# Two-layer hybrid decoder on one core: up projection of the feed-forward part by four feature tiles at a time instead of two

## The chip, the cores and the metric

One core of a Trainium2 chip runs the whole kernel. The metric is the device time of one execution in microseconds (us), the median of the timed runs. Engines: PE is TensorE's matmul, PEld its weight load, DVE VectorE, ACT ScalarE, POOL GpSimd, SP SyncE, which issues the DMAs.

## The reference

Two layers act on a residual stream x of 256 tokens by 2048 features, all in float32. In each layer x gets the output of a mixer (three kinds of attention), then that of a cross attention, then that of the feed-forward part, in which the change lies:

```python
h = rms_norm(x, ffn_norm[l])
u = h @ ffn_w_up[l]                       # 2048 x 11008
up = jnp.pad(u, ((0, 0), (CONV_WIDTH - 1, 0), (0, 0)))
cw = ffn_conv_w[l]
uc = (cw[0] * up[:, :-2] + cw[1] * up[:, 1:-1] + cw[2] * up[:, 2:] + ffn_conv_b[l])
g, val = jnp.split(uc, 2, axis=-1)
x = x + (jax.nn.silu(g) * val) @ ffn_w_down[l]   # 5504 x 2048
```

## The kernel before

Products are made in a rounded float32 format in three parts. A weight piece is loaded by SP into a buffer of tag `raw`; ACT rounds it to `hi` (L98) and DVE subtracts to get `lo` (L100), both in `halves`, called from `load_split`. There are four `raw`, four `hi` and three `lo` buffers of 1 MB each, so a piece's `lo` can be written once PE has left the piece three before it. The activations lie split in the same way: a tile `h3[k]` holds, for one of 16 k-tiles (KT) of 128 features, 256 columns of rounded tokens and 256 of the rest. A matmul of `hi` with all 512 columns (L283) and one of `lo` with the first 256 (L285) make the three parts.

Up projection has 86 feature tiles of 128 in each layer (NF = 43 gates and 43 values). `up_acc` makes the sums of two tiles at a time in two banks of the pool tag `mm` (`pmm`, four banks; the other four have the tag `at`, `pat`). A piece holds 8 k-tiles by 256 columns (`EIGHTS`); for each k-tile come two hi matmuls, then two lo. One k-tile of two feature tiles is called a step below, and 8 steps use up a piece. After every four k-tiles `tick` lets waiting generators run (small sums of the norm factor, parking, weight sums), in an order that counts ticks.

`up_tiles` reads the sums: ACT copies one half of the bank (L1189), DVE adds the other (L1192) and multiplies by the norm factor R (L1193), ACT applies the last convolution tap and the bias (L1194), DVE the two other taps (L1195, L1197). `gate` applies silu on ACT (L1205) and multiplies gate and value on DVE (L1206) into a tile of two neighbouring feature tiles, a pair. For 13 of the pairs (`SEVEN`) down projection uses a seven-product scheme. Such a pair is parked: DVE makes differences (L316 to L318), ACT and DVE round and split (L305, L306, two of each for a pair) and SP writes four tiles to DRAM (L324). For the same pairs `add_up` loads weights of the down projection (L334), DVE adds them (L338) and SP writes the sums to DRAM (L342), paced over the up stage by `todo`. `fetch` later loads a parked pair and one sum again (L355, L359), and is called twice near the end of the up stage, then once for each such pair in `down` (products at L375 to L377, weights at L384 to L386 and L405).

Each engine's instructions are ordered by a scheduler when the program is built; that order is fixed on the chip. Tiles of the tag `k` (`slot`, 38 buffers) hold activations and loads, those of the tag `t` (`tmp`, 7) short-lived values.

## Time and profile before

| What | us |
|---|---|
| median of 3 timed runs | 2463.83 (2463.75 to 2463.97) |
| the profiled execution, its own time | 2463.87 |
| its span, first to last instruction | 2462.1 |
| PE busy in the span | 2454.1 |
| DVE busy | 2009.5 |
| ACT busy | 1414.0 |
| up projection, first layer, about | 537 to 1016 |

The up stage of the second layer lies at about 1760 to 2238 us, and down projection follows each. A busy time is the union of an engine's instructions; matmuls overlap in the record, so the distance from one start to the next, and not the length of one, tells their pace. The same holds for DVE and ACT, whose instructions overlap by some 0.08 us. Idle time of an engine counts only where the chain that ended last goes through it.

### The profile page before, as it was taken

The numbers are of one execution on the slowest core, as the hardware profiler recorded it, in microseconds if no ns is written. First come the engines' busy times: TensorE is split into PE (matmuls) and PEld (weight loads), VectorE is DVE, ScalarE is ACT, GpSimd is POOL, SyncE is SP. The second block draws the span as 40 slices with busy tenths as digits, with TensorE's granted clock in tenths as the row PEclk, the third lists the DMA queues.
The fourth block names the chain that finished last, engine by engine and source line by source line (L and its number), as shares of the span: only waits on it lengthen the run. The fifth ranks groups of instructions, "written<-read, shape, count | busy, mean of one in ns | idle before, by whom it ended". The sixth has DMA issues, their size and how long they took to land.

```text
span 2462.1 us, 35930 instructions
## 1 busy us (share of the span) xinstructions
PE 2454.1 (100%) x13288; PEld 2110.8 (86%) x13288; DVE 2009.5 (82%) x3190; ACT 1414.0 (57%) x1860; POOL 156.2 (6%) x170
## 2 busy tenths in 40 slices
PE   9999999999999999999999999999999999999999
PEld 8788888898888888888887888888988888888887
DVE  7886767778888887899968877776888888878898
ACT  6555566465555555566655555655555555556664
POOL 2301101010000000000031011010100000000000
PEclk9999999999999999999999999999999999999999
DMA  8555556469999898898964555564799999988996
GB/s 281 169 179 162 167 168 221 167 195 319 298 298 315 292 301 263 298 377 293 352 208 154 172 171 159 170 219 141 233 309 301 302 300 304 300 259 314 349 344 240
DMA packets 465444, 619.39 MB, mean 252 GB/s; under 512 B 21182, under 2 KB 334068, under 8 KB 465268
## 3 DMA queue, kind: packets, MB, share of 16 engines
q1 hardware_dynamic: 465268, 617.10, 75.4%
q8 instruction: 104, 1.70, 0.3%
q14 instruction: 72, 0.59, 0.1%
HBM read 558.30 MB, written 58.72 MB: 251 GB/s over the span
## 4 chain that ended last, share of the span: by engine, by line
PE 98%; DVE 1%; issue 0%; DMA 0%; ACT 0%; SPq 0%; POOL 0%; POOLq 0%
PE mm L283 31%; PE mm L285 16%; PE mm L247 10%; PE mm L252 10%; PE mm L248 10%; PE mm L375 4%; PE mm L376 4%; PE mm L377 4%; PE at L376 2%; PE at L377 2%; PE at L375 2%; PE at L690 1%; PE mm L281 1%; PE mm L280 1%; PE at L789 0%
## 5 line engine op out<-in xcount | busy, mean ns | idle before, releaser
L100 DVE TENSOR_TENSOR lo<-raw,hi 128x2048 fp32r<-128x2048 f32 (+4 forms) x466 | 994.5, 2136 | 268.1 <-PE mm L252 109.1
L98 ACT ACTIVATE hi<-raw 128x2048 fp32r<-128x2048 f32 (+4 forms) x466 | 825.5, 1774 | 521.4 <-PE mm L248 198.7
L283 PE MATMUL mm<-k,hi 128*128 128x512 f32 x3008 | 946.1, 396 | 0.0
L285 PEld LDWEIGHTS mm<-k,lo 128*128 128x128 f32 x3136 | 584.9, 188 | 133.5
L285 PE MATMUL mm<-k,lo 128*128 128x256 f32 x3136 | 616.5, 278 | 0.0
L283 PEld LDWEIGHTS mm<-k,hi 128*128 128x128 f32 x3008 | 458.4, 189 | 0.4 <-DVE k L208 0.2
L247 PE MATMUL mm<-hi,k 128*128 128x512 f32 (+2 forms) x1152 | 431.2, 374 | 1.2 <-ACT hi L98 0.8
L248 PE MATMUL mm<-hi,k 128*128 128x512 f32 (+2 forms) x1152 | 423.5, 368 | 0.0
L252 PE MATMUL mm<-lo,k 128*128 128x512 f32 (+2 forms) x1148 | 422.0, 368 | 0.3 <-DVE lo L100 0.3
L247 PEld LDWEIGHTS mm<-hi,k 128*128 128x128 f32 x1152 | 216.8, 188 | 38.5 <-issue 4.8
L252 PEld LDWEIGHTS mm<-lo,k 128*128 128x128 f32 x1148 | 216.0, 188 | 36.9 <-DVE lo L100 0.7
L248 PEld LDWEIGHTS mm<-hi,k 128*128 128x128 f32 x1152 | 217.2, 189 | 32.0
L1194 ACT ACTIVATE t<-t,cw 128x256 f32<-128x256 f32 x172 | 94.3, 595 | 134.1 <-DVE t L1193 134.1
L1195 DVE SCALAR_TENSOR_TENSOR t<-t,cw 128x255 f32<-128x255 f32 x172 | 81.8, 480 | 30.9 <-ACT t L1194 30.9
L375 PE MATMUL mm<-hi,a 128*128 128x512 f32 x272 | 106.2, 390 | 0.4 <-DVE k L419 0.4
L376 PE MATMUL mm<-hi,a 128*128 128x512 f32 x272 | 105.8, 389 | 0.0
L377 PE MATMUL mm<-lo,a 128*128 128x512 f32 x272 | 100.2, 389 | 0.0
L338 DVE TENSOR_TENSOR k<-k 128x512 f32<-128x512 f32 x104 | 69.3, 687 | 24.7 <-DMA k<-in_ffn_w_down_dram 24.0
L1197 DVE SCALAR_TENSOR_TENSOR t<-t,cw 128x254 f32<-128x254 f32 x172 | 81.8, 480 | 3.0
L375 PE MATMUL at<-hi,k 128*128 128x512 f32 x208 | 80.9, 389 | 0.0
L376 PE MATMUL at<-hi,k 128*128 128x512 f32 x208 | 80.9, 389 | 0.0
L283 PE MATMUL mm<-a,hi 128*128 128x512 f32 x256 | 80.8, 396 | 0.0
(247 smaller groups left out, 2854.0 us busy)
## 6 DMA issues: line engine op xcount, KB each, us to landing
raw<-in_ffn_w_up_dram SPq DMA_DIRECT2D x168, 1024.0 KB, 6.1
raw<-in_w_in_dram SPq DMA_DIRECT2D x152, 512.0 KB, 4.7
k<-parked SPq DMA_DIRECT2D x184, 256.0 KB, 6.1
k<-in_ffn_w_down_dram SPq DMA_DIRECT2D x156, 256.0 KB, 6.5
raw<-in_ffn_w_down_dram SPq DMA_DIRECT2D x32, 1024.0 KB, 7.4
raw<-in_ffn_w_down_dram SPq DMA_DIRECT2D x56, 512.0 KB, 6.3
summed<-k SPq DMA_DIRECT2D x104, 256.0 KB, 3.9
parked<-a SPq DMA_DIRECT2D x104, 256.0 KB, 5.0
```

The costliest lines, as they stand in the source:

```text
L98: rounded[0] = nc.scalar.activation(hi[:, v, :], src[:, v, :], AF.Copy)
L100: nc.vector.tensor_tensor(lo[:, v, :], src[:, v, :], hi[:, v, :].bitcast(F32), OP.subtract)
L247: nc.tensor.matmul(o, lhsT=xh, rhs=hi[:, j, :], start=first, stop=False)
L248: nc.tensor.matmul(o, lhsT=xl, rhs=hi[:, j, :], start=False, stop=False)
L252: ins = nc.tensor.matmul(o, lhsT=xh, rhs=lo[:, j, :], start=False, stop=last)
L283: nc.tensor.matmul(outs[i], lhsT=w[0][i], rhs=acts[k], start=first, stop=False)
L285: ins = nc.tensor.matmul(own[i], lhsT=w[1][i], rhs=acts[k][:, :S], start=False, stop=last and (i == 1 or not whole))
L375: nc.tensor.matmul(bank[q], lhsT=x[0], rhs=w[0], start=first, stop=False)
L376: nc.tensor.matmul(bank[q], lhsT=x[1], rhs=w[0], start=False, stop=False)
L377: return nc.tensor.matmul(bank[q], lhsT=x[0], rhs=w[1], start=False, stop=left[q] == 0)
L1194: nc.scalar.activation(v, u, AF.Identity, scale=cw[:, 2, f:f + 1], bias=cw[:, 3, f:f + 1])
L1195: nc.vector.scalar_tensor_tensor(v[:, 1:], u[:, :S - 1], cw[:, 1, f:f + 1], v[:, 1:], op0=OP.mult, op1=OP.add)
```

## The change

Up projection goes by four feature tiles. A weight piece has four k-tiles by 512 columns, 1 MB as before. For each k-tile there are four hi matmuls, then four lo. The gate tiles of a group of four use the four `mm` banks, its value tiles the four `at` banks, in turn. Evacuated gates wait for their values in `k` tiles instead of `t` tiles. Groups start at tiles 0, 4, ..., 36; the pair 40 and 41 and the last tile 42 keep pieces of 8 k-tiles by 256 columns. Pacing of `add_up` is called before the gates and before the values of a group. `fetch` is called after tile 41 rather than 39.

```diff
-        def up_sums(fs):
-            return fs, up_acc(up, [(fs[0] * P, 2 * P)] if fs[1] == fs[0] + 1 else [(f * P, P) for f in fs], h3)
-
-        def up_tiles(fs, outs):
+        def up_sums(fs, new):
+
+            n = len(fs)
+            runs = [(fs[0] * P, n * P)] if fs[-1] == fs[0] + n - 1 else [(f * P, P) for f in fs]
+            outs = [new() for _ in fs]
+            for k0 in range(0, KT, 16 // n):
+                m = 16 // n
+                hi, lo = load_split([up[:, k0:k0 + m, c:c + w] for c, w in runs], m, n * P)
+                for j in range(m):
+                    k = k0 + j
+                    for i in range(n):
+                        nc.tensor.matmul(outs[i], lhsT=hi[:, j, i * P:(i + 1) * P], rhs=h3[k], start=k == 0, stop=False)
+                    for i in range(n):
+                        ins = nc.tensor.matmul(outs[i][:, :S], lhsT=lo[:, j, i * P:(i + 1) * P], rhs=h3[k][:, :S],
+                                               start=False, stop=k == KT - 1)
+                    if (j + 1) * n % 8 == 0:
+                        tick(ins)
+            return fs, outs
+
+        def up_tiles(fs, outs, new=tmp):
 
             res = []
-            uvs = [tmp() for _ in fs]
+            uvs = [new() for _ in fs]
...
-        for f in range(0, NF - 1, 2):
-            while todo and (total - len(todo)) * (NF - 5) < total * (f + 2):
+        def pace(f):
+            while todo and (total - len(todo)) * (NF - 5) < total * f:
                 step(add_up(dn, *todo.pop(0)))
-            us = [up_sums([f, f + 1])]
+
+        for f in [*range(0, NF - 4, 4), NF - 3, NF - 1]:
+            fs = list(range(f, min(f + 4 if f < NF - 3 else f + 2, NF)))
+            pace(f + 2)
+            if len(fs) == 1:
+                gs = up_tiles(*up_sums([f, NF + f], pmm))
+                gate(f, *gs)
+                break
+            us = up_sums(fs, pmm)
             if f:
-                gs = up_tiles(*us.pop())
-            us.append(up_sums([NF + f, NF + f + 1]))
+                gs = up_tiles(*us, new=slot)
+            pace(f + 4)
+            vs = up_sums([NF + v for v in fs], pat)
             if not f:
-                gs = up_tiles(*us.pop(0))
-            vs = up_tiles(*us.pop())
-            gate(f, gs[0], vs[0])
-            gate(f + 1, gs[1], vs[1])
-            if f == NF - 5:
+                gs = up_tiles(*us, new=slot)
+            vs = up_tiles(*vs)
+            for v, a, b in zip(fs, gs, vs):
+                gate(v, a, b)
+            if f == NF - 7:
                 wanted.extend((i, g) for g in range(D // GW) for i in pairs_of(g) if i in SEVEN)
+            if f == NF - 3:
                 for _ in range(2):
                     fetch()
-        gs = up_tiles(*up_sums([NF - 1, 2 * NF - 1]))
-        gate(NF - 1, gs[0], gs[1])
```

Before and after, each engine has the same number of instructions. Three places in the built order show what moves. In the changed program the up matmuls are L1192 (hi) and L1194 (lo), the evacuation L1205 and L1208 to L1213, and the gate's product L1222. Numbers in names tell buffers' uses apart.

PE, in the middle of the up stage of the first layer, one k-tile and the start of the next, before:

```order
L283 MATMUL mm_6729<-k_5261,hi_6783 128x512
L283 MATMUL mm_6730<-k_5261,hi_6783 128x512
L285 MATMUL mm_6729<-k_5261,lo_6784 128x256
L285 MATMUL mm_6730<-k_5261,lo_6784 128x256
L283 MATMUL mm_6729<-k_5262,hi_6783 128x512
L283 MATMUL mm_6730<-k_5262,hi_6783 128x512
```

and in the changed program:

```order
L1192 MATMUL mm_6709<-k_5179,hi_6777 128x512
L1192 MATMUL mm_6710<-k_5179,hi_6777 128x512
L1192 MATMUL mm_6711<-k_5179,hi_6777 128x512
L1192 MATMUL mm_6712<-k_5179,hi_6777 128x512
L1194 MATMUL mm_6709<-k_5179,lo_6778 128x256
L1194 MATMUL mm_6710<-k_5179,lo_6778 128x256
L1194 MATMUL mm_6711<-k_5179,lo_6778 128x256
L1194 MATMUL mm_6712<-k_5179,lo_6778 128x256
```

The matmul's width changes after every four instead of every two, and four banks take turns instead of two.

DVE, where pair 5 (tiles 10 and 11) is gated and parked, before:

```order
L1206 TENSOR_TENSOR k_6718<-t_6704,t_6612 128x256
L1197 SCALAR_TENSOR_TENSOR t_6705<-t_6705,cw_132 128x254
L100 TENSOR_TENSOR lo_6890<-raw_6887,hi_6889 128x2048
L1206 TENSOR_TENSOR k_6718<-t_6705,t_6613 128x256
L316 TENSOR_TENSOR t_6753<-k_6718 128x256
L317 TENSOR_TENSOR t_6753<-t_6753,k_6718 128x128
L306 TENSOR_TENSOR a_6774<-k_6718,a_6773 128x512
L318 TENSOR_TENSOR t_6753<-k_6718,t_6753 128x128
L338 TENSOR_TENSOR k_6723<-k_6723,k_6724 128x512
L306 TENSOR_TENSOR a_6806<-t_6753,a_6805 128x512
L338 TENSOR_TENSOR k_6725<-k_6725,k_6724 128x512
L100 TENSOR_TENSOR lo_6955<-raw_6952,hi_6954 128x2048
```

and in the changed program, where pairs 4 and 5 (`k_6693` and `k_6698`) are gated together, from the last gate on:

```order
L1222 TENSOR_TENSOR k_6698<-t_6668,k_6460 128x256
L306 TENSOR_TENSOR a_6760<-k_6693,a_6759 128x512
L316 TENSOR_TENSOR t_6739<-k_6698 128x256
L306 TENSOR_TENSOR a_6768<-k_6698,a_6767 128x512
L317 TENSOR_TENSOR t_6739<-t_6739,k_6698 128x128
L338 TENSOR_TENSOR k_6703<-k_6703,k_6704 128x512
L318 TENSOR_TENSOR t_6739<-k_6698,t_6739 128x128
L338 TENSOR_TENSOR k_6705<-k_6705,k_6704 128x512
L306 TENSOR_TENSOR a_6800<-t_6735,a_6799 128x512
L100 TENSOR_TENSOR lo_6876<-raw_6873,hi_6875 128x2048
L306 TENSOR_TENSOR a_6808<-t_6739,a_6807 128x512
L100 TENSOR_TENSOR lo_6952<-raw_6949,hi_6951 128x2048
```

Before, a weight piece's L100 stands between the evacuation of two tiles and their park; in the change the evacuation of four tiles, four gates, both parks but one instruction and a weight sum stand between one L100 and the next. The L100 ahead of these rows is that of the third piece after the group whose sums are read.

SP, at the end of the up stage of the first layer, from the last weight pieces on, before:

```order
L222 DMA raw_10023<-in_ffn_w_up_dram 128x8x128 x2
L405 DMA raw_10080<-in_ffn_w_down_dram 128x2x1024
L355 DMA k_9753<-parked_5895 128x512
L355 DMA k_9754<-parked_5897 128x512
L355 DMA k_9755<-parked_5929 128x512
L355 DMA k_9756<-parked_5931 128x512
L359 DMA k_9761<-summed_5507 128x512
```

and in the changed program, some rows further on:

```order
L386 DMA raw_10207<-summed_5515 128x512
L384 DMA raw_10258<-in_ffn_w_down_dram 128x1024
L385 DMA raw_10258<-in_ffn_w_down_dram 128x512
L386 DMA raw_10258<-summed_5691 128x512
L355 DMA k_9962<-parked_5897 128x512
L355 DMA k_9963<-parked_5899 128x512
L355 DMA k_9964<-parked_5931 128x512
L355 DMA k_9965<-parked_5933 128x512
L359 DMA k_9970<-summed_5509 128x512
```

The loads of the first parked pair move from behind down's first weight piece to behind its fifth, `raw_10258`, which takes the buffer of the first, `raw_10080`, once that one is split.

## Rows read from the trace of the kernel before

**Rows 1.** The head of the page: the span, and busy time, share of the span and instructions of each engine.

```profile
span 2462.1 us, 35930 instructions
...
PE 2454.1 (100%) x13288; PEld 2110.8 (86%) x13288; DVE 2009.5 (82%) x3190; ACT 1414.0 (57%) x1860; POOL 156.2 (6%) x170
```

**Rows 2.** Windows inside the up stage of the first and of the second layer: start and end, length, then busy time and instructions of PE, PEld, DVE, ACT and POOL, the granted clock, the DMA engines' share and GB/s.

```profile
541.00:1014.00 473.00, 473.00 (x2721) 412.79 (x2720) 403.30 (x605) 264.02 (x329) 1.74 (x1) 1.00 0.91 298
...
1764.00:2130.00 366.00, 366.00 (x2106) 319.47 (x2105) 313.17 (x470) 203.32 (x251) 1.75 (x1) 1.00 0.92 302
```

**Rows 3.** The chain of work that ended last, shares of the span by engine and by line.

```profile
PE 98%; DVE 1%; issue 0%; DMA 0%; ACT 0%; SPq 0%; POOL 0%; POOLq 0%
PE mm L283 31%; PE mm L285 16%; PE mm L247 10%; PE mm L252 10%; PE mm L248 10%; PE mm L375 4%; PE mm L376 4%; PE mm L377 4%; PE at L376 2%; PE at L377 2%; PE at L375 2%; PE at L690 1%; PE mm L281 1%; PE mm L280 1%; PE at L789 0%
```

**Rows 4.** Groups by line and shape, 545 to 1010 us, the two up matmuls: count, busy us, mean ns of one, idle us of the engine before them.

```profile
L283 PE MATMUL mm<-k,hi 128*128 128x512 f32 x1333 | 418.9, 395 | 0.0
L285 PE MATMUL mm<-k,lo 128*128 128x256 f32 x1334 | 262.1, 278 | 0.0
```

**Rows 5.** Timeline of PE in the up stage: start us, length of the merged row, instruction, count.

```profile
700.01 0.63 PE L283 MATMUL mm<-k,hi 128*128 128x512 f32 x2
700.47 0.40 PE L285 MATMUL mm<-k,lo 128*128 128x256 f32 x2
...
705.58 0.62 PE L283 MATMUL mm<-k,hi 128*128 128x512 f32 x2
```

**Rows 6.** Timeline of PE in down projection, 512-wide matmuls only; from the first row to the last lie seven of them.

```profile
1099.94 0.39 PE L375 MATMUL at<-hi,k 128*128 128x512 f32 x1
...
1100.62 0.39 PE L375 MATMUL mm<-hi,k 128*128 128x512 f32 x1
...
1101.53 0.39 PE L376 MATMUL at<-hi,k 128*128 128x512 f32 x1
```

**Rows 7.** Timeline of PE in the cross attention's value projection, 256-wide matmuls only; from the first row to the last lie twelve.

```profile
507.86 0.28 PE L247 MATMUL mm<-hi,k 128*128 128x256 f32 x1
...
509.30 0.28 PE L247 MATMUL mm<-hi,k 128*128 128x256 f32 x1
```

**Rows 8.** The chain that ended last in order of time, in the up stage of the second layer: start us, length, what. Twenty-four steps lie from the first row to the last, each with one such hi pair.

```profile
1820.70 0.47 PE mm L283 x2
1821.39 0.46 PE mm L283 x2
...
1837.42 0.47 PE mm L283 x2
```

**Rows 9.** Timeline of DVE near the end of the first up stage; the distance between starts is what an instruction or a pair takes.

```profile
988.44 0.42 DVE L1206 TENSOR_TENSOR k<-t 128x256 f32<-128x256 f32 x1
988.78 0.48 DVE L1197 SCALAR_TENSOR_TENSOR t<-t,cw 128x254 f32<-128x254 f32 x1
...
991.83 0.43 DVE L316 TENSOR_TENSOR t<-k 128x256 f32<-128x256 f32 x1
992.29 0.29 DVE L317 TENSOR_TENSOR t<-t,k 128x128 f32<-128x128 f32 x1
992.50 0.69 DVE L306 TENSOR_TENSOR a<-k,a 128x512 fp32r<-128x512 f32 x1
993.10 0.28 DVE L318 TENSOR_TENSOR t<-k,t 128x128 f32<-128x128 f32 x1
...
996.90 0.75 DVE L1192 TENSOR_TENSOR t<-mm,t 128x256 f32<-128x256 f32 x2
997.56 0.75 DVE L1193 TENSOR_TENSOR t<-t,k 128x256 f32<-128x256 f32 x2
998.23 0.68 DVE L306 TENSOR_TENSOR a<-k,a 128x512 fp32r<-128x512 f32 x1
998.83 0.87 DVE L1195 SCALAR_TENSOR_TENSOR t<-t,cw 128x255 f32<-128x255 f32 x2
999.62 0.87 DVE L1197 SCALAR_TENSOR_TENSOR t<-t,cw 128x254 f32<-128x254 f32 x2
1000.41 2.28 DVE L100 TENSOR_TENSOR lo<-raw,hi 128x2048 fp32r<-128x2048 f32 x1
1002.61 1.89 DVE L306 TENSOR_TENSOR a<-k,a 128x512 fp32r<-128x512 f32 x3
```

**Rows 10.** Timeline of DVE, four additions of down weights (L338) on end.

```profile
548.15 2.48 DVE L338 TENSOR_TENSOR k<-k 128x512 f32<-128x512 f32 x4
```

**Rows 11.** Waits, 545 to 1010 us: who waited for whom, us in total, times, longest us.

```profile
DVE t L1195 <- ACT t L1194: 15.3, 38, 0.6
DVE k L338 <- DMA k<-in_ffn_w_down_dram: 12.5, 14, 2.4
DVE lo L100 <- PE mm L285: 9.5, 8, 2.0
...
DVE a L306 <- ACT a L305: 0.7, 1, 0.7
```

**Rows 12.** The fetch: SP's timeline at the end of the first up stage, and, from the source line L355, the time from issue to landing over the whole run.

```profile
985.84 2.39 SPq L355 DMA_DIRECT2D k<-parked  x4
988.27 0.53 SPq L359 DMA_DIRECT2D k<-summed  x1
...
DMA to landing us min/median/max: 5.3/6.1/8.9
```

**Rows 13.** Timeline of PE, the first matmul of down projection in the first layer.

```profile
1016.29 0.40 PE L375 MATMUL mm<-hi,a 128*128 128x512 f32 x1
```

## The prediction

> **What bounds the kernel now.** I read the page's head first, then windows by stage, then the chain of waits, then single stretches of the timeline. The head has TensorE (PE) busy for 2454.1 of 2462.1 us [rows 1]. Busy says little of a pipelined engine, so the stage that changes was looked at by itself: in the two stretches of up projection, 473 and 366 us, PE is busy for the whole of both at a granted clock of 1.00, while VectorE (DVE) has 403.3 and 313.2 us of work, about 85%, and the DMA engines' share is 0.91 and 0.92 [rows 2]. 98% of the chain that ended last is PE, and its first two entries are the matmuls of `up_acc`, 31% and 16% [rows 3]. The groups of that stage give an idle time of 0.0 before both kinds of up matmul [rows 4]. So nothing is waited for there, neither weights nor split halves nor banks, and the stage can get shorter only if the matmuls themselves follow each other faster.
>
> How fast they follow is read from start times. One k-tile for two feature tiles is two 512-wide matmuls (hi) and two 256-wide ones (lo). From 700.01 to 705.58 us eight such steps pass: 0.696 us a step [rows 5]. Where 512-wide matmuls stand alone, seven take 1.59 us, 0.2271 us each, also where the bank changes from `at` to `mm` [rows 6]. Where 256-wide ones stand alone, twelve take 1.44 us, 0.120 us each [rows 7]. Two of each would make 0.6942 us. Over a longer stretch of the chain, 1820.70 to 1837.42, twenty-four steps take 16.72, 0.6967 us each [rows 8]. The mix thus costs 0.0025 us a step beyond what its parts cost alone.
>
> **The change part by part.** The profiled run took 2463.87 us (span 2462.1 and 1.8 around it), 0.04 above the median of the three timed runs, 2463.83.
>
> *Instructions.* Each engine issues as many as before: the weight pieces are still 172 of 1 MB over both layers, and evacuations, gates, parks and weight sums keep their number. The sum holds only orders and waits.
>
> *Order on PE.* Four hi, then four lo, in place of two and two, for 40 feature tiles of each half: 10 groups x 2 halves x 16 k-tiles x 2 layers = 640 new steps, each in place of two old ones. The other three tiles keep the old pattern. Size now changes twice in eight matmuls, not twice in four. The bank changes at every matmul, before and after, and [rows 6] shows no price on that. So I put the 0.0025 us to the change of size and halve it: an old pair of steps takes 2 x 0.6967 = 1.3934, a new step 1.3884 + 0.0025 = 1.3909. **-0.0025 x 640 = -1.6 us.** Bounds: the rows don't show which of two neighbouring matmuls holds its time. By start times a pair of hi holds 0.46 or 0.47, 0.465 on the mean [rows 5, 8], which leaves 0.232 of the step to a pair of lo. If four hi kept 0.2325 each and four lo took the 0.120 of [rows 7], a new step would take 1.410, +0.0166 x 640 = +10.6 us. If four hi took 0.2271 and four lo kept 0.116, it would take 1.3724, -13.4 us. Both need the two sizes to be priced against each other, so I take the value next to [rows 6] and [rows 7], where each size has one price, with a weight load for every matmul and a change of bank among them. By the difference of the two, 0.1071 us for 256 columns, about 13 ns of every matmul don't grow with its width. The Trainium skill, "TensorE: Matmul & The Clock Gate", section "Wait — 56ns, not 53.3ns?", gives every matmul a fixed cost, about 2.5 ns, beside its columns, whatever stands next to it. The trace agrees on a fixed part but shows 13 ns and a price of the mix besides. By that page alone this term would be 0 and the sum 2463.9.
>
> *Evacuation in fours (DVE).* This is where the change could lose. DVE's order shows that at a group's end three further split pieces (`lo` has three buffers) are ahead of the evacuation, the third of them starting only when PE has left the group. Then come four tiles' sums, the gates, the parks and the weight sums, and only then the next piece. Worst are the groups in which both activation pairs are parked, pairs (4,5), (10,11) and (16,17), three in a layer. There, from start times in [rows 9] and [rows 10]: the third piece 2.20; four tiles at 2.91 for two (0.66 + 0.67 + 0.79 + 0.79) 5.82; four gates at 0.34, 1.36; two parks at 0.46 + 0.21 + 0.28, 1.90; three of their four roundings at 0.60, 1.80; two weight sums at 0.62, 1.24; and the next piece itself 2.20. Sum 16.5 us after the group's end. PE needs that piece after three others, 3 x 8 x 0.6967 = 16.7, and reads its lo only after four hi, 0.93 later: 17.6. So 1.1 us are spare, where the old order, with two tiles between pieces, had DVE itself wait for free `lo` buffers, 9.5 us in eight waits [rows 11]. **I take 0.** Upper bound: in one such place the longest wait seen for a weight sum's load, 2.4, for a rounding, 0.7, and two hand-overs from ScalarE at 0.6 [rows 11], 4.3 less 1.1 = 3.2 us, six times, 19 us. Below nothing isn't possible, PE has no wait to lose.
>
> *Weight pieces.* Runs of 2 KB in place of 1 KB may land sooner. PE has no idle time in the stage [rows 4], so there is none for earlier weights to take away: 0.
>
> *Banks.* Sums go to `mm` and `at` in turn, and each set is read while the other fills, 22.3 us. 0. In the first group `at` also holds the two small sums of the norm factor; the later one is made a tick, 16 matmuls or 2.8 us, before the second half begins, whose fourth tile is the first to need its bank.
>
> *The fetch ahead of down (SP).* `fetch` is called after tile 41, not 39, and SP now has ten loads of parked tiles behind three loads whose buffer comes free with down's first split. That split takes the `lo` buffer of the piece third from the end, free 2 x 8 x 0.6967 = 11.1 us before down starts, and lasts 2.2. From 8.9 before down, three issues and five more at 0.61 (four in 2.43 [rows 12]) put the first set's last issue at 4.0 before, landing at 2.1 after by the median of 6.1, at 4.9 by the longest of 8.9 [rows 12]. PE reads it after 24 matmuls of down's first pair, 24 x 0.2271 = 5.45. Covered by 3.3 us, or 0.5; without that cover each microsecond later is one of PE's. **0.** Before, those loads were asked for from 985.8, and down began at 1016.3 [rows 12, 13].
>
> Sum: 2463.87 - 1.6 = **2462.3 us**, 0.06% under the time before. A measurement of this kernel can't tell less than 0.2%, 4.9 us, from no change.
>
> **The rivals.**
> - *Late split pieces, slower.* DVE, 85% busy [rows 2], works in bursts twice as long, and a weight sum that waits for its load stands ahead of a piece. It decides once more than 1.1 us of waits fall between the group's end and the fourth piece. With one wait of 2.4 and the work as counted, PE stops 1.3 us at six places: 2462.3 + 7.8 = 2470.1; by the bound, 2481. For: the margin is the thinnest of the sum, and 14 such waits, 12.5 us, lie in one layer [rows 11]. Against: in most of them DVE had nothing else due, and the new loads are asked for well ahead. 0.12.
> - *The fetch lands late, slower.* If SP is held until the last piece's end, the first set lands at 2.1 + 8.9 = 11.0, 5.5 us late in each layer: 2473.3. For: the lead shrinks from 30 us to 9. Against: the margin above. 0.04.
> - *Lo in fours is slow, slower.* The first bound of the PE term: 2463.87 + 10.6 = 2474.5. For: four lo in turn leave the next weights half the time that hi leave. Against: lo alone stand at 0.120 in [rows 7], little more than here. 0.04.
> - *Hi in fours is fast, faster.* The second bound: 2463.87 - 13.4 = 2450.5. For: 512-wide matmuls are 0.2325 apart here and 0.2271 elsewhere. Against: the step's sum fits its parts to 0.4%, so what hi loses lo has gained. 0.07.
> - *The order is free.* The 13 ns of a matmul [rows 6, 7], and the 0.0025 us of a step too, may belong to single matmuls whatever stands next to them; no matmul is added, so 2463.9. It lies on the forecast's side, whose own range is 2460.7 (all of the 0.0025 gone) to 2468.
>
> **How the numbers follow.** The forecast, with the case of a free order, has 0.73, which leaves 0.07 faster and 0.20 slower. The predicted time is the forecast's, 2462.3. For eight in ten the range takes in the forecast's own cases from 2460 and the nearer half of late pieces, up to 2470.
>
> **What would show it.** Right: steps of eight matmuls 1.390 to 1.392 us apart, idle 0.0 before the up matmuls, and before the fourth piece after tiles 8 to 11, 20 to 23 and 32 to 35 DVE done with less than 2 us to spare. Wrong: PE idle there until `lo` (late pieces), or idle in down after its first 24 matmuls (fetch); a step of 1.41 or 1.37 us would name the PE term. A change beyond 4.9 us without either would mean that the price of a matmul depends on something these rows don't show.

## The result, and the profile after

The change makes the kernel slower: 2478.89 us (2477.44 to 2480.14, four runs) against 2463.79 (2463.17 to 2463.97, four runs), a ratio of 1.0062 (95% interval 1.0044 to 1.0079). The forecast was 2462.3 us with a range up to 2470. The profiled execution took 2479.76 us. In the changed kernel the up matmuls are L1192 (hi) and L1194 (lo), and the evacuation is L1205 to L1213.

The page's head of the changed kernel (counterpart of [rows 1]), and its chain that ended last, by line (of [rows 3]):

```profile
span 2478.0 us, 35933 instructions
...
PE 2464.9 (99%) x13288; PEld 2120.0 (86%) x13288; DVE 1995.6 (81%) x3190; ACT 1412.9 (57%) x1860; POOL 156.4 (6%) x170
```

```profile
PE mm L1192 13%; PE at L1192 13%; PE mm L247 10%; PE mm L252 10%; PE mm L248 9%; PE mm L1194 7%; PE at L1194 6%; PE mm L283 5%; PE mm L375 4%; PE mm L376 4%; PE mm L377 4%; PE mm L285 3%; PE at L375 2%; PE at L376 2%; PE at L377 2%; DVE lo L100 1%
```

The number of instructions on PE, DVE, ACT and POOL is that of before. PE is busy for 10.8 us more with the same 13288 matmuls, so some of them hold it longer, and the span has grown by 5.1 us beyond that, so PE also stands idle somewhere. By the first up matmul and the first of down projection, the up stage takes 488.0 us in the first layer (535.77 to 1023.81) and 489.7 in the second (1765.20 to 2254.91); before it took 480.2 and 481.9. These 7.8 us in each layer are nearly all of the 15.9 us by which the two profiled spans differ.

**The start of the stage.** The longest of PE's waits in the changed kernel (us in total, times, longest us), with no counterpart before:

```profile
PE mm L1192 <- DVE xT L524: 5.2, 4, 2.2
```

PE's timeline there, first layer (start us, length, instruction, count, idle time ahead and its releaser), and DVE's beside it:

```profile
535.77 0.63 PE L1192 MATMUL mm<-k,hi 128*128 128x512 f32 x2
536.76 0.50 PE L1192 MATMUL mm<-k,hi 128*128 128x512 f32 x1 [0.35 <-DVE xT L524]
...
541.36 0.50 PE L1192 MATMUL mm<-k,hi 128*128 128x512 f32 x1 [2.24 <-DVE xT L524]
...
542.84 1.06 PE L1194 MATMUL mm<-k,lo 128*128 128x256 f32 x4
543.70 1.91 PE L1192 MATMUL mm<-k,hi 128*128 128x512 f32 x4
545.41 0.81 PE L1194 MATMUL mm<-k,lo 128*128 128x256 f32 x4
```

```profile
536.02 0.68 DVE L524 TENSOR_TENSOR xT<-mm,xT 128x512 f32<-128x512 f32 x1
536.62 2.27 DVE L100 TENSOR_TENSOR lo<-raw,hi 128x2048 fp32r<-128x2048 f32 x1
538.82 1.89 DVE L210 SCALAR_TENSOR_TENSOR k<-xT,gains,k 128x256 fp32r<-128x256 f32 x2
540.63 0.68 DVE L524 TENSOR_TENSOR xT<-mm,xT 128x512 f32<-128x512 f32 x1
```

The first group asks for all four `mm` banks at once. Two of them still hold the last sums of the cross attention's residual, which DVE adds to `xT` (L524) in its own order: the last one at 540.63, behind a split of 2.27 us (L100) and two subtractions that take 1.89 together (L210). PE goes on with three tiles until it needs the fourth bank. In the kernel before, the first two tiles used the two banks that were already free, and the other two were wanted 11 us later. After the stop the four hi that start at 543.70 hold PE for 1.71 us instead of 0.93. The windows show why (us, then busy time of PE, PEld, DVE, ACT, POOL, granted clock, DMA share, GB/s):

```profile
539.00:542.00 3.00, 0.76 (x4) 0.60 (x4) 3.00 (x4) 1.64 (x3) 1.03 (x1) 1.00 0.56 168
542.00:546.00 4.00, 4.00 (x16) 3.41 (x16) 3.65 (x4) 1.08 (x3) 1.72 (x1) 0.57 0.97 318
546.00:550.00 4.00, 4.00 (x24) 3.47 (x24) 3.75 (x4) 1.62 (x1) 0.00 (x0) 1.00 0.58 220
...
1771.00:1775.00 4.00, 4.00 (x14) 3.39 (x14) 4.00 (x4) 1.20 (x3) 1.72 (x1) 0.57 1.03 345
```

The granted clock has a mean of 0.57 over 4 us, which costs 0.43 x 4 = 1.7 us; by the trace's records it is 0.50 from 542.36 to 545.77, 3.41 us, and 1.00 around that. The Trainium skill, "TensorE: Matmul & The Clock Gate", section "What's actually happening", has half rate as the gate's resting state, entered after an idle window of about 3.4 us that runs freely. The trace agrees on the half rate (1.71 against 0.93 us) and on the 3.4 us; but the window before, 538.95 to 542.36, was idle for 2.24 us of it and not throughout. Waits and slow clock are 0.35 + 2.24 + 1.7 = 4.3 us in a layer.

**The steady step.** The chain in order of time, up stage of the first layer (start us, length, what; counterpart of [rows 8]), and the windows that answer to [rows 2]:

```profile
812.30 0.93 PE mm L1192 x4
...
855.80 0.93 PE mm L1192 x4
```

```profile
541.00:1014.00 473.00, 472.64 (x2690) 413.08 (x2691) 387.93 (x591) 259.08 (x325) 1.72 (x1) 1.00 0.84 288
1771.00:2137.00 366.00, 366.00 (x2082) 319.89 (x2082) 298.02 (x452) 198.86 (x246) 1.72 (x1) 1.00 0.84 294
```

Thirty-one steps of eight matmuls lie between 812.30 and 855.80: 1.4032 us each, where two old steps took 1.3934 and I had forecast 1.3909. PE is busy without a break, so this is no wait: 0.0098 x 640 = 6.3 us in both layers. Together with the start, 2 x 4.3 + 6.3 = 14.9 of the 15.9 us. DVE has less to do in the same time than before (388 of 473 us), and the DMA share fell to 0.84, without any effect on PE.

### The profile page after: what moved, and what is told of

Its sections match the earlier page's. It is cut to its first block, busy times and chain, and to the rows that moved or that the text cites. A ratio compares the mean times of both kernels' runs of the same rounds, so it can differ in the third digit from the quotient of the medians.

```text
span 2478.0 us, 35933 instructions
## 1 busy us (share of the span) xinstructions
PE 2464.9 (99%) x13288; PEld 2120.0 (86%) x13288; DVE 1995.6 (81%) x3190; ACT 1412.9 (57%) x1860; POOL 156.4 (6%) x170
## 4 chain that ended last, share of the span: by engine, by line
PE 97%; DVE 2%; issue 0%; ACT 0%; POOL 0%; ACTq 0%; POOLq 0%
PE mm L1192 13%; PE at L1192 13%; PE mm L247 10%; PE mm L252 10%; PE mm L248 9%; PE mm L1194 7%; PE at L1194 6%; PE mm L283 5%; PE mm L375 4%; PE mm L376 4%; PE mm L377 4%; PE mm L285 3%; PE at L375 2%; PE at L376 2%; PE at L377 2%; DVE lo L100 1%
## 5 line engine op out<-in xcount | busy, mean ns | idle before, releaser
L100 DVE TENSOR_TENSOR lo<-raw,hi 128x2048 fp32r<-128x2048 f32 (+4 forms) x466 | 993.3, 2136 | 348.2 <-PE mm L252 109.1
L1192 PE MATMUL mm<-k,hi 128*128 128x512 f32 x1408 | 393.7, 397 | 5.2 <-DVE xT L524 5.2
L1192 PE MATMUL at<-k,hi 128*128 128x512 f32 x1344 | 369.5, 394 | 0.0
L1192 PEld LDWEIGHTS mm<-k,hi 128*128 128x128 f32 x1408 | 239.4, 190 | 36.2 <-DVE xT L524 6.9
L1192 PEld LDWEIGHTS at<-k,hi 128*128 128x128 f32 x1344 | 228.5, 189 | 29.4
L1194 PEld LDWEIGHTS mm<-k,lo 128*128 128x128 f32 x1408 | 222.1, 190 | 33.1
L1194 PEld LDWEIGHTS at<-k,lo 128*128 128x128 f32 x1344 | 208.5, 189 | 30.1
L1194 PE MATMUL mm<-k,lo 128*128 128x256 f32 x1408 | 230.6, 282 | 0.0
L1194 PE MATMUL at<-k,lo 128*128 128x256 f32 x1344 | 216.2, 281 | 0.0
L283 PE MATMUL mm<-k,hi 128*128 128x512 f32 x256 | 81.5, 400 | 0.0
```

The lines of the kernel that those rows point to most:

```text
L100: nc.vector.tensor_tensor(lo[:, v, :], src[:, v, :], hi[:, v, :].bitcast(F32), OP.subtract)
L283: nc.tensor.matmul(outs[i], lhsT=w[0][i], rhs=acts[k], start=first, stop=False)
L1192: nc.tensor.matmul(outs[i], lhsT=hi[:, j, i * P:(i + 1) * P], rhs=h3[k], start=k == 0, stop=False)
L1194: ins = nc.tensor.matmul(outs[i][:, :S], lhsT=lo[:, j, i * P:(i + 1) * P], rhs=h3[k][:, :S], start=False, stop=k == KT - 1)
```

## The experiments

All times are medians, and each ratio is to the kernel before, run on the same chip beside it (medians 2463.2 to 2463.9). In the diffs, hi and lo stand for the two matmul statements. The theory was: the stop at the start costs some 9 us, the order in fours the rest. The rivals put the one or the other on the pieces, on the change of bank or on the evacuation.

**start_pair.** Groups 0-1, then fours from tile 2 to 41, then 42:

```diff
-        for f in [*range(0, NF - 4, 4), NF - 3, NF - 1]:
+        for f in [0, *range(2, NF - 1, 4), NF - 1]:
...
```

> The changed kernel, but the up stage begins with the pair of tiles 0 and 1 (its gates in two mm banks, its values in two at banks); the groups of four start at tile 2. Theory (the start): the first group of four asks for all four mm banks while the last two sums of the cross attention's residual still stand in them, and the granted clock drops after that stop; without it the waits for xT (5.2 us) and the windows at a clock of 0.57 go, about 4.6 us a layer, so 2469 to 2471 us, with steps of eight matmuls still 1.403 us. Rival (the start is dear for another reason, such as pieces of four k-tiles or the norm factor's sums): 2477 to 2479 us, and a stop stays somewhere in the first 15 us of the stage.

Measured: 2489.41 us, 1.0102 (1.0087 to 1.0117), a miss. The bank wait was gone, but another had come. PE's waits, and DVE's timeline before tile 2 could start:

```profile
PE mm L1192 <- DVE k L1208: 9.5, 2, 5.3
```

```profile
556.21 0.69 DVE L338 TENSOR_TENSOR k<-k 128x512 f32<-128x512 f32 x1 [1.40 <-DMA k<-in_ffn_w_down_dram]
558.09 0.69 DVE L338 TENSOR_TENSOR k<-k 128x512 f32<-128x512 f32 x1 [1.18 <-DMA k<-in_ffn_w_down_dram]
...
562.95 0.76 DVE L1208 TENSOR_TENSOR k<-mm,k 128x256 f32<-128x256 f32 x2 [1.63 <-ACT k L1205]
```

My edit paced `add_up` twice within the first pair, so more weight sums were made at the start than in either kernel: six additions (L338) up to 565 us, against four. SP stood for 11.9 us at stores that wait for such sums (L342 for L338), with weight pieces behind them; ACT waited 12.2 us for a piece, and the evacuation of the first gates is queued behind its rounding. So the group at tile 2 found the banks of tiles 0 and 1 still full. In each layer a granted clock of 0.50 for 6.83 us followed; PE was busy for 5.2 and 5.6 us of them, which costs half as much more, 2.6 and 2.8 us. The run doesn't tell the theories apart; `pair_ends` below mends it.

**two_two.** The change with only the order of its matmuls undone:

```diff
-                    for i in range(n): hi ...
-                    for i in range(n): lo ...
+                    for h in range(0, n, 2):
+                        for i in (h, h + 1): hi ...
+                        for i in (h, h + 1): lo ...
```

> The changed kernel with its matmuls ordered hi hi lo lo for two tiles, then the same for the other two; pieces, banks and evacuation stay in fours. Theory (the order in fours makes the step dear): eight matmuls take 2 x 0.6967 = 1.393 us again instead of 1.403, 640 x 0.0099 = 6.3 us less, 2472 to 2473 us. Rival (four banks in use or pieces of 512 columns make it dear): 1.403 us and 2478 to 2480 us.

Measured: 2472.43 us, 1.0034 (1.0022 to 1.0046). The chain shows old steps again, 18 in 12.54 us, 0.6967 each:

```profile
856.37 0.47 PE mm L1193 x2
...
868.91 0.47 PE mm L1193 x2
```

So the order alone makes the step dear; four banks, pieces of 512 columns and evacuation in fours leave it at 1.393. Of the 8.5 us that are left above the kernel before, the stop explains 6.4: 5.0 us of waits for L524 in two layers, and a slow clock in the second one alone (a mean of 0.66 over 4 us, 1.4 us). The cause of the remaining 2.1 us is not shown.

The same stop lowers the clock in one layer and not in the other because of where it falls. In every trace the half clock in the up stage begins and ends on a grid of 3.413 us, by the trace's clock records; in the change at 542.36, 545.77, 1771.16 and 1774.57, where 1771.16 - 542.36 is 360 such steps. Windows of that grid, two of the change and four of `two_two`, the columns as above:

```profile
538.95:542.36 3.41, 1.17 (x6) 0.91 (x6) 3.41 (x4) 2.04 (x4) 1.08 (x1) 1.00 0.60 192
542.36:545.77 3.41, 3.41 (x12) 2.87 (x11) 3.29 (x4) 0.49 (x2) 1.72 (x1) 0.50 0.95 302
```

```profile
537.50:540.91 3.41, 2.12 (x10) 1.51 (x10) 3.41 (x3) 3.24 (x4) 1.71 (x1) 1.00 0.56 210
540.91:544.33 3.42, 2.16 (x12) 1.95 (x13) 3.42 (x5) 1.44 (x3) 0.60 (x1) 1.00 1.00 344
1762.89:1766.30 3.41, 1.51 (x8) 0.93 (x7) 3.41 (x4) 2.58 (x3) 1.71 (x1) 1.00 0.55 182
1766.30:1769.71 3.41, 2.85 (x9) 2.46 (x10) 3.41 (x3) 1.44 (x3) 1.29 (x1) 0.50 0.99 333
```

In the change PE is idle for 2.24 us of one window (3.41 less 1.17), and the next window has half the clock. In the first layer of `two_two` a boundary cuts the stop in two, 1.29 and 1.26 us, and the clock stays; in the second 1.90 us lie in one window, and it drops. In all seventeen traces a window at full clock with 1.90 us of idle time or more is followed by half the clock, and one with 1.88 or less is not (this one in `before_ones`, at its end).

**bank_runs.** The same matmuls ordered by bank, four hi and four lo of one tile, then the next tile:

```diff
-                for j in range(m): for i in range(n): hi; for i in range(n): lo
+                for i in range(n): for j in range(m): hi; for j in range(m): lo
```

> The changed kernel with its matmuls ordered by bank: within a piece, for each tile its four hi, then its four lo, all into one bank. Size changes as often as in the change, the bank once in eight matmuls instead of at each. Theory A (a change of bank is what makes hi 0.2325 us instead of the 0.2271 of other stages): eight matmuls take 4 x 0.2271 + 4 x 0.120 = 1.388 us, 9.5 us less, and the first group needs its third and fourth bank 2.8 and 4.2 us later, so most of the start's 9 us goes too: 2460 to 2463 us. Theory B (runs of four of one size are the dear thing, whatever the bank): steps stay at 1.403 us, only the start is better: 2469 to 2472 us.

Measured: 2473.35 us, 1.0037 (1.0024 to 1.005). Eight steps take 11.22 us, 1.403 each:

```profile
700.18 1.09 PE L1191 MATMUL at<-k,hi 128*128 128x512 f32 x4
...
711.40 1.09 PE L1191 MATMUL at<-k,hi 128*128 128x512 f32 x4
```

Theory B: a change of bank has no price. The stop shrank to 1.3 us in each layer, at a clock of 1.00. The total is 1.4 us above theory B's range; a part of the stop stayed.

**one_one.** hi and lo of a tile directly behind each other:

```diff
                     for i in range(n):
                         hi
-                    for i in range(n):
                         lo
```

> The changed kernel with hi and lo of a tile directly behind each other, the bank changing after every second matmul and the size at every one. Theory A (a change of size has a price): eight size changes instead of two in a step, 1.41 us or more, 2483 us and above. Theory B (runs of one size are dear, fours dearer than twos): below the 1.393 of the pairs, about 1.385 us, 2467 to 2470 us. Theory C (a change of bank has a price): half as many changes, about 1.396 us, 2474 us.

Measured: 2472.66 us, 1.0037 (1.0027 to 1.0047), but spread from 2469.59 to 2488.55, and the profiled execution was the longest. Its step was 1.413 us. No theory covers both; it is taken up again below.

**pair_ends.** The start with a pair, mended:

```diff
-        for f in [*range(0, NF - 4, 4), NF - 3, NF - 1]:
+        for f in [0, *range(2, NF - 5, 4), NF - 5, NF - 3, NF - 1]:
...
-            pace(f + 4)
+            if len(fs) == 4:
+                pace(f + 4)
```

> The changed kernel with a pair at the start (tiles 0 and 1), fours for tiles 2 to 37 and pairs 38, 40 at the end; the second pacing of weight sums is left out of the pairs, so that no more sums are asked for in the first 22 us than before. The first try of a start with a pair moved the stop instead of removing it: SP stood for 11.9 us at a store that waits for a weight sum, with the next weight piece behind it, and PE waited 4.4 and 5.4 us for the evacuation at tile 2. Theory (the start is dear by its banks alone): no stop of PE over 0.6 us from 530 to 600 us nor at the start of down, clock 1.00 throughout, about 9 us less than the change, and 64 of the 640 steps back in pairs, 0.6 us: 2468.5 to 2470.5 us. Rival (a first group of four is dear in itself, wherever it stands: evacuated gates in k tiles, pieces of four k-tiles): a stop at tile 2 again, 2475 us or more.

Measured: 2470.85 us, 1.0029 (1.0018 to 1.004), 8.0 us less than the change, 0.6 of which belong to the 64 steps that are pairs again, and 0.35 above the theory's range. No wait of PE over 0.4 us is left in the stages, and the start is full:

```profile
536.00:541.00 5.00, 5.00 (x30) 4.35 (x29) 5.00 (x6) 3.25 (x4) 1.74 (x1) 1.00 0.69 222
541.00:546.00 5.00, 5.00 (x30) 4.37 (x29) 5.00 (x6) 3.24 (x4) 1.74 (x1) 1.00 0.93 313
```

The stop was one of banks; a group of four that starts at tile 2 brings none of its own. The step stays at 1.403 us, so 576 of them explain 5.6 of the 7.4 us above the kernel before.

**pair_ends_two.** Both undone: `pair_ends` with the order of `two_two`.

> The same, and the matmuls in the order hi hi lo lo. Theory (stop at the start and order in fours are all of the 15 us): 2463 to 2465 us, no difference to the kernel before. Rival (something else in fours has a price, such as the evacuation, the pieces or the later fetch): 2466 us or more.

Measured: 2465.33 us, 1.0008 (0.9999 to 1.0018), not to be told from the kernel before, and between the theory's range and the rival's. Pieces of 512 columns, eight banks in turn, evacuation in fours, gates in `k` tiles and the later fetch are still in it. The rest of 1.9 us, about as much as in `pair_ends`, lies within the interval; it contains one wait of 0.9 us for an evacuated gate in the second layer (`PE mm L1193 <- DVE k L1209`).

**before_fours.** The reverse: the kernel before with nothing but the order changed, four hi of two k-tiles, then their four lo, in all groups but the first of a layer.

```diff
+                for j0 in range(0, 8, 2):
+                    for j in (j0, j0 + 1): for i in range(2): hi
+                    for j in (j0, j0 + 1): for i in range(2): lo
```

> The kernel before, only the order of its matmuls changed, in all groups but the first of each layer: four hi (two k-tiles of two feature tiles), then their four lo. Two banks, pieces of 256 columns, evacuation and pacing as before. Theory (the order in fours alone makes the step dear): 1.403 us for eight against 1.393, 672 of them, 6.6 us: 2469.5 to 2471 us. Rival (fours are dear only with four banks or with pieces of four k-tiles): 1.393 us, 2463 to 2464 us.

Measured: 2470.11 us, 1.0026 (1.0016 to 1.0037), as expected of the order alone. From 856.75 to 867.98 us eight steps pass, 1.404 each:

```profile
856.75 0.93 PE mm L1188 x4
...
867.98 0.93 PE mm L1188 x4
```

**Other orders.** Four runs ask what in the order has the price. In the changed kernel, hi in runs of three and one with lo in twos:

```diff
+  order of one k-tile, (hi = 1, tile): (1,0) (1,1) (1,2) (0,0) (0,1) (1,3) (0,2) (0,3)
```

> The changed kernel with the eight matmuls of a k-tile in the order hi hi hi lo lo hi lo lo: hi in runs of three and one, lo in runs of two. Theory A (only the run of lo counts: in pairs a lo holds 115 ns, in fours 119, alone 120, while hi holds 233 in both): 1.393 us for eight, 2472 to 2473 us with the stop at the start. Theory B (the run of hi counts, or equal runs do): 1.400 us or more, 2477 us and above.

Measured: 2481.13 us, 1.007 (1.0055 to 1.0085), with steps of 1.400 us. Theory A falls, theory B holds: lo in twos are not enough. The total is above what that step gives (2472.4 + 640 x 0.0067 = 2476.7); 2.8 us of it lie behind the second up stage, 221.2 us from the first matmul of down projection to PE's last against 218.4 in the change, for a cause that was not pursued.

In the kernel before, in all sums but the first two gate tiles of a layer, runs of eight into one bank, runs of 32 (all hi of a group, then all lo), and single ones:

```diff
+ before_runs:   for i in range(2): for j in range(8): hi; for j in range(8): lo
+ before_halves: for both pieces: for i in range(2): for j in range(8): hi;  then the same for lo
+ before_ones:   for j in range(8): for i in range(2): hi; lo
```

> The kernel before, only the order changed, in all groups of the up stage but the first: within a piece of eight k-tiles by 256 columns eight hi into one bank, then its eight lo, then the same for the other bank. No change to banks, pieces, evacuation or pacing. Theory A (a run of lo costs, its first one 111 ns, each further one 120): eight matmuls take 4 x 0.233 + 4 x 0.119 = 1.408 us against 1.393, 2 layers x 336 of them, 10 us more: 2473 to 2475 us. Theory B (the price in fours came from four k-tiles or four banks): 1.393 us or less, 2461 to 2465 us. If hi in the middle of a run of eight stand 0.227 us apart, as in other stages, then the higher 0.233 belongs to the change of size, and the sum is 1.387 us, 2460 us.

> The kernel before, in all groups but the first: all 32 hi of a group of two tiles (both its pieces), then its 32 lo. Theory A (a change from one size to the other and back costs at most what runs of eight showed, 8 x 2.5 = 20 ns above the 346.6 ns of a hi and a lo that stand alone): in runs of 32 that is 0.6 ns for each hi and lo, eight matmuls 1.389 us against 1.393, 3 us less: 2460 to 2462 us. Theory B (the price goes on rising with the run, as from twos to fours): 1.397 us or more, 2466 us and above.

> The kernel before, in all groups but the first: hi and lo of a tile directly behind each other, the size changing at every matmul. With the whole change this order took 1.413 us for eight in the one profiled execution, which was 16 us longer than the median of that kernel. Theory A (the profiled step holds): 1.413 us, 13 us more: 2476 to 2478 us. Theory B (it was that execution alone, and the median tells the order's price): the median less the 8.5 us of the stop at the start, 2463 to 2465 us, no difference.

Measured: `before_runs` 2466.84 us, 1.0017 (1.0007 to 1.0026), between its two theories; `before_halves` 2462.55, 0.9996 (0.9987 to 1.0005), theory A in its step, with a wait of 0.7 us for an evacuation in the second layer; `before_ones` 2476.72, 1.0054 (1.004 to 1.0068), theory A. One cycle of `before_halves` and the start of the next, from its chain:

```profile
803.63 7.28 PE mm L1191 x32
810.91 3.83 PE mm L1194 x32
814.75 7.28 PE mm L1191 x32
```

From one hi run to the next are 11.12 us, 1.390 for each eight matmuls. The table has, for each order, how long a hi and a lo hold PE, as the mean distance from a matmul's start to the next one's between 600 and 960 and between 1830 and 2180 us of the traces, and four of each:

| Order | hi, ns | lo, ns | eight matmuls, us |
|---|---|---|---|
| single, higher level (`before_ones`) | 236.6 | 116.8 | 1.413 |
| single, lower level (`before_ones_all`, below) | 231.7 | 115.0 | 1.387 |
| twos (kernel before) | 233.1 | 115.2 | 1.393 |
| three and one, lo in twos | 232.3 | 117.7 | 1.400 |
| fours (the change, `bank_runs`, `before_fours`) | 232.3 | 118.5 | 1.403 |
| eights | 230.1 | 119.1 | 1.397 |
| thirty-twos | 227.5 | 119.8 | 1.389 |
| each alone [rows 6, 7] | 227.1 | 120.0 | 1.388 |

In a run of eight hi the first five hold 233.5, 235.8, 228.3, 232.5 and 230.9 ns and the last three 226.6; a lo holds 113.6 in first place and 120 from the third on; in runs of thirty-two the first places are the same. So each size does go to its price alone, lo at once and hi only after five, and the time between is what a change costs: about 21 ns for there and back in eights, 17 in fours, 3.5 in twos and, at the lower level, nothing in single ones (346.7 ns for a hi and a lo, against 346.6; in `one_one_b`, below, also at the lower level, they hold 230.0 and 116.7, with the same sum).

**The two levels.** The single order was run once more with the whole change, and then entered without a stop.

> The changed kernel with hi and lo of a tile behind each other, once more. Its times lay between 2469.6 and 2488.6 us, while the kernel before in the same order keeps to 2476.3 to 2477.8 us, of which the step of 1.413 us explains all. Theory A (the step itself differs between executions when four banks take turns): a profiled execution of about 2471 us shows steps of about 1.390 us. Theory B (the step stays 1.413 us, and it is the stop at the start or the granted clock that differs): 1.413 us in any execution, 2485 us or more.

Measured: five times, 2471.57 us median, one of them 2479.38. The profiled execution took 2471.82. The chain of the earlier profile of this same program and of this one (twenty-seven pairs of hi and lo in the first, twenty-eight in the second):

```profile
800.09 0.24 PE at L1192
...
809.63 0.24 PE at L1192
```

```profile
800.07 0.23 PE at L1192
...
809.78 0.23 PE mm L1192
```

One pair takes 0.3533 us in the first and 0.3468 in the second; eight matmuls 1.413 and 1.387. Theory A holds: it is the step that differs between two executions of one program. From 600 us on, and from 1830 on in the second layer, each profile has one level to the end of the stage. Times near 2471.5, 2480 and 2488 fit none, one or both layers at the higher level, 320 x 0.026 = 8.3 us each.

> The changed kernel with a pair at the start and pairs at the end, and hi and lo of a tile behind each other; no stop at the start. Theory A (the level is set by how the stage is entered, and the stop is what gave the lower): 1.413 us for eight, 688 x 0.0199 = 13.7 us above the kernel before: 2476 to 2479 us. Theory B (four banks in turn, or the straight entry, give the lower level): 1.387 us, 688 x 0.0068 = 4.7 us below: 2458 to 2461 us, faster than both.

> The kernel before with hi and lo of a tile behind each other in all groups, the first of each layer too, so that the order is entered straight from the residual's 256-wide matmuls and not from a group of pairs. Theory A (entered without a stop it stays at the higher level): 1.413 us, 2476 to 2479 us. Theory B (the group of pairs ahead set the higher level): 1.387 us, 2458 to 2461 us.

> The kernel before in the same order, but the first of the eight k-tiles of each piece in the order hi hi lo lo, in all groups but the first. Theory A (the level is a phase that any disturbance can change): steps between 1.387 and 1.413 us that change from piece to piece, 2460 to 2475 us. Theory B (the higher level is where this order always settles without a stop): 1.410 us, 2474 to 2476 us.

`before_ones_all` is `before_ones` with the order in the first group of each layer too:

```diff
-            return fs, (up_acc if fs[0] == 0 else up_runs)(up, ...)
+            return fs, up_runs(up, ...)
```

Measured: 2460.42 us (2459.56 to 2460.87, ten runs), 0.9985 (0.9975 to 0.9995): faster than both kernels, by 3.3 us against the kernel before. The time is that of theory B. From its page and its chain, where 28 pairs pass in 9.71 us:

```profile
PE 2450.4 (100%) x13288; PEld 2109.4 (86%) x13288; DVE 2010.4 (82%) x3190; ACT 1417.3 (58%) x1860; POOL 157.6 (6%) x170
```

```profile
800.09 0.23 PE mm L1187
...
809.80 0.23 PE mm L1187
```

But the group of pairs ahead, which theory B names, is not what sets the level. `before_ones_all` itself begins at the higher one in both layers, and changes to the lower one after four small matmuls of the norm factor (L1172). PE's timeline there, first layer; fourteen pairs lie between the first two rows, and fourteen between the last two:

```profile
550.82 0.40 PE L1187 MATMUL mm<-k,hi 128*128 128x512 f32 x1
...
555.76 0.40 PE L1187 MATMUL mm<-k,hi 128*128 128x512 f32 x1
...
556.12 0.61 PE L1172 MATMUL at<-t,ones 128*128 128x128 f32 x4
...
556.91 0.40 PE L1187 MATMUL mm<-k,hi 128*128 128x512 f32 x1
...
561.76 0.40 PE L1187 MATMUL mm<-k,hi 128*128 128x512 f32 x1
```

A pair takes 0.353 us ahead of them and 0.346 behind. The traces of four other runs with single matmuls show the same kind of place: `pair_ends_one` changes to the lower level there in both layers; `one_one` goes down after the norm factor's other four matmuls (L506, 552.57) and up again after L1172 (561.35), and likewise in the second layer; `one_one_b` goes down after L506 in the first layer and in the slow clock behind the stop in the second; `before_ones` passes L1172 at 555.10 and stays at the higher level. So in these traces the level changes only where something breaks the stream near its start, and then holds for the rest of the stage. Why one break changes it and another doesn't is open.

`pair_ends_one` took 2461.09 us, at the edge of theory B, with three of ten runs at 2468.9 to 2470.1, as if one layer had taken the higher level; over all runs 1.0 (0.9989 to 1.001). `ones_with_a_two` took 2476.04, 1.0051 (1.0036 to 1.0066), theory B: a change of order in every piece doesn't leave the higher level.

## Why the prediction was wrong

- *Instructions, 0.* Right: the same counts on every engine that computes.
- *Order on PE, -1.6.* The first step that failed, in sign as in size: +6.3 us. It put the 0.0025 us of a mixed step on the change of size and took a fixed price for each change, so half as many changes had to cost half. `before_fours` and `two_two` show the order alone at 1.403 us in either kernel. A change there and back costs 3.5 ns in twos, but 17 in fours and 21 in eights: in twos it is hardly paid. The row that I held to be the whole price [rows 8] was the cheap case. The bound of +10.6 had the sign and the place right (hi at 0.2325 and lo at 0.120; measured 0.2323 and 0.1185) and the size too high; as a rival it had a chance of only 0.04. The fixed cost of a matmul that the Trainium skill gives ("TensorE: Matmul & The Clock Gate", section "Wait — 56ns, not 53.3ns?") would have made this term 0. The runs don't agree: the same eight matmuls took between 1.387 and 1.413 us, by their order and, in the single order, at two levels.
- *Evacuation in fours, 0.* Right, and close: after tiles 8 to 11, where 1.1 us were forecast to spare, DVE finished the fourth piece at 692.59, and PE began to read its lo four hi, 0.93 us, after 692.85, so 1.2 us were spare. From the group's end at 676.01 DVE needed 16.6 us for its work (16.5 forecast), so the sum was right and not only its outcome; the five other such places have 1.2 us too. PE waits for no lo in the up stage. The rival of late split pieces is refuted.

```profile
690.31 2.28 DVE L100 TENSOR_TENSOR lo<-raw,hi 128x2048 fp32r<-128x2048 f32 x1
```

```profile
692.38 0.63 PE L1194 MATMUL mm<-k,lo 128*128 128x256 f32 x4
692.85 0.40 PE L1192 MATMUL mm<-k,hi 128*128 128x512 f32 x1
```

- *Weight pieces, 0.* Right: DMA share 0.84 for 0.91, and no effect.
- *Banks, 0.* The second step that failed, about 8.6 us by the trace. That "each set is read while the other fills, 22.3 us" holds for every group but the first. There the `mm` banks are not handed over by an earlier group of the stage but by the residual, whose last two sums DVE reads up to 4.9 us after the stage's first matmul. I looked at the `at` banks of the first group, for the norm factor, and not at its `mm` banks. The wait is 2.6 us a layer, and the granted clock that drops behind it costs up to 1.7 more. `pair_ends` takes wait and slow clock away and leaves pieces, evacuation and the order in fours; it is 8.0 us shorter.
- *The fetch, 0.* Right: the first set was asked for from 1016.56 to 1018.98, 4.8 us before down (forecast 4.0), and PE doesn't wait there in the first layer.
- *The sum.* 2463.87 - 1.6 became 2463.8 + 6.3 + 8.6 = 2478.7, measured 2478.89. Of the two terms that failed, one took its price from the old pattern alone, and the other looked at the steady case and not at the start. With both undone, `pair_ends_two`, the difference is down to 1.9 us, which the interval doesn't tell from none.

Open: why the price of a mixed run depends on its length in this way, why the single order has two levels, and what decides at a break which one follows. The runs show that it is so, not why.

## What to carry to other kernels

When a group takes more banks or buffers at a time, write down who held each of them last at the first group, with that engine's queue ahead of the release, and not only how the groups hand over to each other. The price of an order of matmuls isn't the sum of prices of single changes: run the order by itself in the kernel before, as `before_fours` did, before counting on it. Where an order has two levels, one profile doesn't tell which one the timed runs are at; the spread of the times does. And read the step at the start of the stage too, and not in its middle alone, before naming what set the level.

## What the runs showed of the hardware that was not expected

- One program (`one_one`, `one_one_b`) ran its stream of alternate 512- and 256-wide matmuls at 1.387 or at 1.413 us for eight, at a granted clock of 1.00, and kept the level to the end of the stage. The level changed only near the start, at breaks of the stream: at four matmuls of one or of 128 columns, or in the slow clock behind a stop. By their times, all ten runs of `before_ones_all` ended at the lower level and all five of `before_ones` at the higher.
- In runs of eight and of thirty-two, the first five 512-wide matmuls behind 256-wide ones held PE for 228 to 236 ns each, the others for 226.6.
- The granted clock changed on a grid of 3.413 us. It fell to 0.50 for one or two steps of the grid where PE had been idle for 1.90 us or more of one step, and stayed at 1.00, once there, where the idle time in a step was 1.88 or less. So a stop of 2.49 us did no harm in the first layer of `two_two`, where a boundary cut it in two, and lowered the clock in its second layer. The Trainium skill's page on the clock gate ("TensorE: Matmul & The Clock Gate", section "What's actually happening") has a window of this length that runs freely; the traces agree on that, and show that a window need not be idle throughout.
